# A second standing place for gathered cache values in the MLP, two value products per interruption, and the sampled tokens' norm kept in SBUF

## The chip, the cores and the metric

The kernel runs on one core of a Trainium2 chip. TensorE (called PE in the profile) multiplies; its weight loads are listed apart as PEld. VectorE is DVE, ScalarE is ACT, GpSimd is POOL, and SyncE (SP) issues most transfers. Each engine has its own queue of instructions and works it off in order; engines wait for each other through semaphores. The metric is the device time of one execution in microseconds; less is better.

## The reference

One step of a one-layer decoder on 2048 new prompt tokens and on 64 sampled tokens (8 sequences of 8), all in float32:

```python
z = jnp.einsum('bsd,dc->bsc', x, w_in)              # 1024 -> all projections
fox_h = _fox_prompt(fq, fk, fv, flogf)              # causal attention, 8 heads of 64
(C_p, n_p, m_p), m_h = _mlstm_prompt(mq, mk, mv, ig, lf)
...
k_past = cache_k[l][page_table].reshape(DB, past, FOX_HEADS, FOX_HEAD_DIM)
v_past = cache_v[l][page_table].reshape(DB, past, FOX_HEADS, FOX_HEAD_DIM)
...
s_past = jnp.einsum('bqhd,bkhd->bhqk', q, k_past) * scale + Ln + R
p = jax.nn.softmax(jnp.concatenate([s_past, s_new], axis=-1), axis=-1)
o = jnp.einsum('bhqk,bkhd->bqhd', p[..., :P], v_past) + ...   # sampled attention, 8192 past tokens
...
mix = jnp.concatenate([fox_h, mn], axis=-1) @ w_o
x1 = _layer_norm(DN_ALPHA * x + mix, ln1_g, ln1_b)
hid = jnp.square(jax.nn.relu(x1 @ w1))              # 1024 -> 4096
return _layer_norm(DN_ALPHA * x1 + hid @ w2, ln2_g, ln2_b)
```

The sampled attention reads 8 sequences x 64 pages x 128 tokens of keys and as many of values from a paged cache through a page table: 128 MB each.

## The kernel before, in words

The program has these stages, one after the other: A (input projections), B (prompt attention), O (output projection and first norm, `phase_o`), and C (the MLP and second norm, `phase_c`). The large products are written as three float32r matmuls of 512 columns (`mm3`, L162 to L164): an operand is split into a high and a low part, the high parts made by ACT (`split_hi`, L153) and the low ones by DVE or POOL (`split_lo`, L156).

The sampled attention is a generator, `sample_attention`, that is advanced beside all other work. Its 294 steps (`step(n)`) run in stage A up to step 78 and go on from there in O and C. `tick(us)` is called after each piece of the main work with the TensorE time that the piece is worth; when 4.93 us have come together in O and C, one step is emitted. What a step does is fixed by its number n:

- every fourth step (n % 4 == 2): `qk_step`, the scores of four gathered pieces of keys (tile `sQ`, L1826, 16 matmuls of 32 output rows and 256 columns; the trace has two records for each of them, since they are in float32);
- every second step from 38 on: `pv_step`, the value product of one pair of gathered pieces of values, called a pair below (tile `sO`, L1938, 8 matmuls for each half of the pair in the trace, 16 in all);
- at two steps out of eight: `weights`, which turns four blocks of the softmax's result (tile `sT`, L1895) into `PTs`, the stationary operand of the next four pairs;
- gathers: `k_gather` (L1803) fetches one piece of 128 rows x 4 KB by an indirect DMA on POOL's queue, into a ring of six; `v_gather` (L1914) fetches the two pieces of a pair, 1 MB.

`two_sides`, `mm3` and the narrow matmuls share TensorE's queue, so each step that multiplies interrupts the wide matmuls. The interruptions are called runs here: all that stands on PE between two wide matmuls.

A pair of values needs a place in SBUF. The first place is the two `vt` buffers of the attention's own pool. The second is whatever `vx["more"]()` gives at the time: the tiles `vx` of stage O's pool, and in stage C the two landing buffers `xr`, through which the normed rows x1 also come back from DRAM to be turned (`x1_load`, L1249). Since the landing buffers are needed for that at the end of each of the MLP's four blocks, `vx["more"]` is set to `None` from the seventh of the eight passes of a block to the end of the eighth, and `take_back` emits attention steps until no pair stands in the second place. With no second place, one pair is gathered and consumed at a time.

Stage C works on four blocks of tokens: 512, 512, 512 and 512 + 64 (the sampled tokens, tile 16). For each block `x1_turn` (L1261) puts x1 transposed into `x1h` and `x1l`, `hidden` makes 256 columns of the hidden layer (tile `ph`), and `output` multiplies them with w2 by a seven-product scheme and adds the results to the rows `ys` (tile `y`, L1452). The rows are loaded from DRAM at the start of a block by DMAs on ACT's queue (L1510) and are normed and stored at the start of the next one. They come from a ring of five tiles (`row`), which stage O uses as well.

The sampled tokens' output projection and first norm (`sampled`, `norm_quick`) are done at the end of the third block, after the attention has ended. The normed rows are written to DRAM (L197), loaded again into a landing buffer to be turned, and loaded a third time as the row tile of the fourth block.

The order of instructions on an engine is set by a scheduler that simulates a timeline; `issue_after` holds an instruction behind another.

## Time and profile before

| | |
|---|---|
| median of 3 runs | 3186.63 us (3184.83 to 3199.43) |
| profiled execution, its time | 3196.47 us |
| its span, first to last instruction | 3194.7 us |
| mean granted TensorE clock | 0.99 |
| PE busy | 3107.4 us, 97% of the span |
| DVE / ACT / POOL busy | 65% / 45% / 28% |
| bytes moved by DMA | 732.58 MB, mean 229 GB/s |
| stage O, from the first wide matmul | about 1300 to 1526 us |
| stage C, blocks 1 to 3, with the attention | about 1526 to 2735 us |
| sampled tokens' projection, norm and turn | about 2735 to 2790 us |
| stage C, block 4 | to the end |

Lines of a timeline read: start, duration, engine, line, operation, tiles (out<-in), shape, count, and in brackets the engine's idle time before and what ended it. Lines of a table of waits read: waiting engine, tile and line, what it waited for, microseconds in total, times, the longest.

### The profile page before, as it was taken

The page shows a single profiled execution, that of the slowest core. Times are in us where ns is not written, and L with a number is a line of the kernel's source. Part 1 is how long each engine was busy: PE and PEld are TensorE (multiplying, and loading weights), DVE is VectorE, ACT ScalarE, POOL GpSimd, SP SyncE. Part 2 cuts the span into 40 slices and gives each one's busy share as a digit, 9 for nine tenths or more (in the row PEclk, how much of TensorE's full clock was granted, in tenths as well). Part 3 has the DMA queues.
Part 4 walks back from the last instruction along what each step waited for, and adds up shares of the span by engine and source line. Part 5 has one row for each costly group of instructions (what it writes and reads, how often), then busy time and mean ns, then how long its engine had stood idle before and what let it go on. Part 6 is the DMA issues. An engine that isn't in the chain of part 4 may idle for free. (4 is left out here: it accounts for less than half of the span.)

```text
span 3194.7 us, 53743 instructions
## 1 busy us (share of the span) xinstructions
PE 3107.4 (97%) x19869; PEld 2442.5 (76%) x19869; DVE 2084.9 (65%) x5025; ACT 1438.9 (45%) x2629; POOL 907.6 (28%) x976
## 2 busy tenths in 40 slices
PE   8999999999999999999999999999999999899998
PEld 8997787787766667777677777777767777698886
DVE  6857467465488787534656568565676665766667
ACT  3343244343387777412444455343444444344442
POOL 0121132423443333476333324333333111000000
PEclk9999999999999999999999999999999999999999
DMA  5565665877787765687877879878779766643231
GB/s 191 153 212 183 236 227 201 285 258 241 239 272 176 196 172 133 228 300 250 318 277 284 303 243 341 302 263 315 294 259 342 277 213 208 209 155 133 100 124 63
DMA packets 323614, 732.58 MB, mean 229 GB/s; under 512 B 63096, under 2 KB 153720, under 8 KB 322456
## 3 DMA queue, kind: packets, MB, share of 16 engines
q1 hardware_dynamic: 235928, 413.36, 39.1%
q0 software_dynamic: 83808, 304.91, 27.4%
q10 hardware_dynamic: 3616, 10.88, 0.9%
q8 instruction: 157, 2.57, 0.3%
q14 instruction: 105, 0.86, 0.1%
HBM read 676.20 MB, written 86.38 MB: 239 GB/s over the span
## 5 line engine op out<-in xcount | busy, mean ns | idle before, releaser
L156 DVE TENSOR_TENSOR wl<-wr,wh 128x1024 fp32r<-128x1024 f32 x300 | 366.0, 1222 | 241.4 <-ACT wh L153 235.4
L153 ACT ACTIVATE wh<-wr 128x1024 fp32r<-128x1024 f32 x300 | 315.8, 1055 | 338.8 <-PE py L164 166.0
L162 PE MATMUL ph<-x1h,wh 128*128 128x512 f32 (+1 forms) x1280 | 455.4, 356 | 0.0
L163 PE MATMUL ph<-x1l,wh 128*128 128x512 f32 (+1 forms) x1280 | 453.7, 355 | 0.2 <-DVE x1l L156 0.2
L164 PE MATMUL ph<-x1h,wl 128*128 128x512 f32 (+1 forms) x1280 | 451.8, 355 | 1.0 <-DVE wl L156 0.8
L1803 POOL DMA_INDIRECT kT<-cache_k,idxK x256 | 276.4, 1080 | 556.5 <-PE sQ L1826 491.5
L162 PE MATMUL py<-wh,hh 128*128 128x512 f32 x900 | 357.9, 402 | 5.6 <-DVE y L1452 3.0
L163 PE MATMUL py<-wl,hh 128*128 128x512 f32 x900 | 354.3, 395 | 0.0
L164 PE MATMUL py<-wh,hl 128*128 128x512 f32 x900 | 351.3, 394 | 0.4 <-DVE hl L156 0.4
L1452 DVE TENSOR_TENSOR y<-y,py 128x512 f32<-128x512 f32 x410 | 277.3, 682 | 101.2 <-PE py L164 97.0
L1914 POOL DMA_INDIRECT vt<-cache_v,idxV x164 | 179.0, 1091 | 399.5 <-PE sO L1938 337.6
L162 PEld LDWEIGHTS ph<-x1h,wh 128*128 128x128 f32 x1280 | 241.6, 189 | 40.4 <-issue 7.4
L164 PEld LDWEIGHTS ph<-x1h,wl 128*128 128x128 f32 x1280 | 240.8, 189 | 37.4 <-issue 3.7
L163 PEld LDWEIGHTS ph<-x1l,wh 128*128 128x128 f32 x1280 | 241.6, 189 | 35.2 <-issue 3.7
L162 PE MATMUL pm<-xh,whi 128*128 128x512 f32 (+2 forms) x640 | 230.9, 361 | 0.0
L164 PE MATMUL pm<-xh,wlo 128*128 128x512 f32 (+2 forms) x640 | 228.5, 357 | 0.0
L163 PE MATMUL pm<-xl,whi 128*128 128x512 f32 (+2 forms) x640 | 227.6, 356 | 0.0
L162 PEld LDWEIGHTS py<-wh,hh 128*128 128x128 f32 x900 | 169.2, 189 | 59.3 <-issue 21.2
L162 PE MATMUL pm<-whi,xh 128*128 128x256 f32 (+4 forms) x624 | 202.2, 325 | 8.9 <-ACT whi L153 8.9
L156 DVE TENSOR_TENSOR wlo<-wra,whi 128x1024 fp32r<-128x1024 f32 (+1 forms) x112 | 139.9, 1251 | 100.7 <-ACT whi L153 100.2
L164 PEld LDWEIGHTS py<-wh,hl 128*128 128x128 f32 x900 | 170.5, 189 | 40.0 <-issue 2.1
L163 PE MATMUL pm<-wlo,xh 128*128 128x256 f32 (+4 forms) x624 | 200.1, 321 | 0.6 <-DVE wlo L156 0.6
(378 smaller groups left out, 6495.7 us busy)
## 6 DMA issues: line engine op xcount, KB each, us to landing
wr<-w SPq DMA_DIRECT2D x200, 512.0 KB
wra<-w_in SPq DMA_DIRECT2D x104, 512.0 KB
wr<-dw SPq DMA_DIRECT2D x96, 512.0 KB
dw<-w POOLq DMA_DIRECT2D x48, 512.0 KB, 7.2
Rb<-dR SPq DMA_DIRECT2D x128, 128.0 KB
kT<-dw SPq DMA_DIRECT2D x28, 512.0 KB
kT<-w SPq DMA_DIRECT2D x25, 512.0 KB
xn<-xp_t SPq DMA_DIRECT2D x16, 512.0 KB
```

What stands on the lines that cost most here:

```text
L153: last["ACT"] = A.activation(dst, src, AF.Copy, scale=scale)
L156: r = (eng or V).tensor_tensor(dst, src, hi.bitcast(F32), op=OP.subtract)
L162: T.matmul(ps, wh, xh, start=first, stop=False, skip_group_check=shared)
L163: T.matmul(ps, wh, xl, start=False, stop=False, skip_group_check=shared)
L164: last["PE"] = T.matmul(ps, wl, xh, start=False, stop=stop, skip_group_check=shared)
L1452: V.tensor_tensor(y, y, ps, op=op)
L1803: G.indirect_dma_start(out=piece(n), out_offset=None, in_=ck, in_offset=IO(ap=idxK[:, b, j // 2, j % 2:j % 2 + 1], axis=0))
L1914: vx["last"] = G.indirect_dma_start(out=vt.rearrange("p f c -> p (f c)"), out_offset=None, in_=cv, in_offset=IO(ap=idxV[:, b, (kt % 4) * 4 ...
```

## The change

The change touches stages O and C only; stages A and B issue the same instructions in the same order.

- The ring of output rows has four tiles and a fifth one, `y5`, of its own. Stage O uses `y5` for every fifth row tile. In stage C the blocks use the four of the ring; `y5` is a half of the second place for gathered values and, after the attention's end, the row tile of the sampled tokens.
- `x1h` and `x1l` are 512 columns wide for the first three blocks and 576 for the fourth, for which their pool is closed and opened again. The 4 KB per partition that this leaves hold `vt2`, the other half of the second place.
- In stage C `vx["more"]` is `second`, which hands out `y5` and `vt2` in turn, and is not withdrawn. `take_back` at the blocks' ends is gone (the one at the end of stage O stays).
- At a step with n % 4 == 2 the pair p and, if its gather was emitted at an earlier step, the pair p + 1 are both multiplied, right behind the step's `qk_step`; the step after next then has no pair left to do. `v_gather` is called at most once per step, at each step that has room, instead of as often as there is room at every second step. `weights` may come one step earlier when the previous four pairs are done.
- The sampled tokens' normed rows stay in `y5`: they are turned from there and are block 4's row tile. The write to DRAM and both loads are gone.

```diff
@@ norm_quick
-            e.dma_start(out[:, h[i]], x[:, h[i]])
+            if out is not None:
+                e.dma_start(out[:, h[i]], x[:, h[i]])
@@ phase C
     def row():
-        return C["py"].tile([128, D], F32, name="y", bufs=5)
+        return C["py"].tile([128, D], F32, name="y", bufs=4)
+
+    def fifth():
+        return C["py"].tile([128, D], F32, name="y5", bufs=1)
+
+    def second():
+
+        C["second"] = not C.get("second")
+        return fifth() if C["second"] else C["px"].tile([128, D], F32, name="vt2", bufs=1)
+
+    def x1_pool():
+
+        es_x1.close()
+        C["px"] = es_x1.enter_context(tc.tile_pool(name="px", bufs=1, side="right", reuse_waits="tile"))
...
         if i == 0 and 0 in halves:
-            C["x"] = (C["px"].tile([128, 8, 576], F32R, name="x1h", bufs=1), C["px"].tile([128, 8, 576], F32R, name="x1l", bufs=1))
+            if t == 12:
+                x1_pool()
+            C["x"] = [C["px"].tile([128, 8, 576 if t == 12 else 512], F32R, name=m, bufs=1) for m in ("x1h", "x1l")]
...
-            xs[t] = row()
+            xs[t] = fifth() if t % 5 == 3 else row()
...
+        x1_pool()
+        vx["more"] = second
...
-            y = row()
+            y = C["y16"] = fifth()
...
-            C["normed"] = norm_quick(y[:64], 64, st, *gb, pc, dx1[S:], SY)
+            C["normed"] = norm_quick(y[:64], 64, st, *gb, pc, None)
...
-                    begun.append(x1_load(CB[ci][i + 2]))
+                    t = CB[ci][i + 2]
+                    begun.append(C["y16"] if t == 16 else x1_load(t))
...
-        vx["more"] = landing
...
                     for t in blk:
+                        if t == 16:
+                            ys[t] = C["y16"]
+                            continue
                         ys[t] = row()
...
-                if p == 6:
-                    vx["more"] = None
...
-                    vx["more"] = landing
...
                 if p == 6 and ci < 3:
-                    take_back()
                     begun = [x1_load(t) for t in CB[ci + 1][:2]]
@@ step
         if p is not None and p < 128:
-            pv_step(p // 16, p % 16, after)
+            due = [p] if p >= vx["done"] else []
+            if n % 4 == 2 and vx["at"].get(p + 1, n) + 1 < n:
+                due.append(p + 1)
+            for p in due:
+                after = pv_step(p // 16, p % 16, after)
+                vx["done"] = p + 1
...
-        for hg in range(2):
-            u = at(n, 36 + hg, 8)
-            if u is not None and u < 32:
-                weights(u // 4, u % 4, hg)
+        u, hg = divmod(vx["turned"], 2)
+        if u < 32 and n >= 36 + hg + 8 * u - (1 if u % 4 and vx["done"] >= 4 * u else 0):
+            weights(u // 4, u % 4, hg)
+            vx["turned"] += 1
...
-        if n >= 35 and (n % 2 == (0 if sole else 1) or not vx["live"]):
-            while v_room():
-                v_gather()
+        if n >= 35:
+            if sole:
+                if n % 2 == 0 or not vx["live"]:
+                    while v_room():
+                        v_gather(n)
+            elif v_room():
+                v_gather(n)
```

How the order moves is shown at three places. The first is TensorE's queue in the middle of the MLP's first block, around two of the attention's steps. Before (rows of L162 to L164 are wide matmuls):

```order
L163 MATMUL ph<-x1l,wh 128x512
L164 MATMUL ph<-x1h,wl 128x512
L1826 MATMUL sQ<-kT,qb 32x256 x16
L1938 MATMUL sO<-vt,PTs 32x256 x8
L162 MATMUL ph<-x1h,wh 128x512
L163 MATMUL ph<-x1l,wh 128x512
```

and 46 rows further on

```order
L163 MATMUL ph<-x1l,wh 128x512
L164 MATMUL ph<-x1h,wl 128x512
L1938 MATMUL sO<-xr,PTs 32x256 x8
L1895 MATMUL sT<-ident,S 128x128 x4
L162 MATMUL py<-wh,hh 128x512
L163 MATMUL py<-wl,hh 128x512
```

The first pair stands in the run of the scores, the second in a run of its own with four transposes.

The same scores and pairs in the changed kernel, whose lines from 197 on have moved (L1845 is the scores' line, L1958 the pairs'; `vt_19301` and `y_19299` are `vt2` and `y5`):

```order
L163 MATMUL ph<-x1l,wh 128x512
L164 MATMUL ph<-x1h,wl 128x512
L1845 MATMUL sQ<-kT,qb 32x256 x16
L1958 MATMUL sO<-vt,PTs 32x256 x8
L1958 MATMUL sO<-vt_19301,PTs 32x256 x4
L1958 MATMUL sO<-y_19299,PTs 32x256 x4
L162 MATMUL ph<-x1h,wh 128x512
L163 MATMUL ph<-x1l,wh 128x512
```

The second pair, which had a run of its own together with four transposes, now follows the first in the scores' run. Over stages O and C the order has 118 runs with narrow matmuls before and 80 now; 60 of the 118 hold one pair and no scores, 11 of the 80 do.

The second place is POOL's queue at the end of the MLP's first block, where the second place was withdrawn before (L179 is a step of the rows' norm). Before:

```order
L1803 DMA kT<-cache_k,idxK 128x1024 x4
L1914 DMA vt<-cache_v,idxV 128x1024 x2
L1914 DMA xr<-cache_v,idxV 128x1024
L179 TENSOR_TENSOR ln_rs<-ln_rs,nhalf 128x1 x2
L1914 DMA vt<-cache_v,idxV 128x1024 x2
L179 TENSOR_TENSOR ln_rs<-ln_rs,nhalf 128x1 x2
L1914 DMA vt<-cache_v,idxV 128x1024 x2
L1803 DMA kT<-cache_k,idxK 128x1024 x4
L1914 DMA vt<-cache_v,idxV 128x1024 x2
L1803 DMA kT<-cache_k,idxK 128x1024 x4
L1914 DMA vt<-cache_v,idxV 128x1024 x2
```

And with the change (L1822 gathers keys, L1934 values):

```order
L1822 DMA kT<-cache_k,idxK 128x1024 x4
L1934 DMA vt<-cache_v,idxV 128x1024 x2
L1934 DMA vt_20721<-cache_v,idxV 128x1024
L1934 DMA y_20719<-cache_v,idxV 128x1024
L1822 DMA kT<-cache_k,idxK 128x1024 x4
L1934 DMA vt<-cache_v,idxV 128x1024 x2
L1934 DMA vt_21001<-cache_v,idxV 128x1024
L1934 DMA y_20999<-cache_v,idxV 128x1024
L179 TENSOR_TENSOR ln_rs<-ln_rs,nhalf 128x1 x3
L1822 DMA kT<-cache_k,idxK 128x1024 x4
L1934 DMA vt<-cache_v,idxV 128x1024 x2
L1934 DMA vt_21260<-cache_v,idxV 128x1024
```

Pairs that were gathered one at a time into `vt` alone are gathered two at a time, and the four gathers of keys stand between two pairs and the next two, here as in the rest of stage C.

The third place is ACT's queue at the start of the MLP's second block, where the block's four rows are loaded. Before:

```order
L1510 DMA y<-dx_71 128x1024
L1434 ACTIVATE hq<-ph 128x512
L1510 DMA y<-dx_71 128x1024 x2
L1435 ACTIVATE hq<-hq 128x512
L1510 DMA y<-dx_71 128x1024
L1897 COPY PTs<-sT 128x4x4x8
L153 ACTIVATE hh<-s 128x512
```

With the change:

```order
L1532 DMA y<-dx_71 128x1024
L1453 ACTIVATE hq<-ph 128x512
L1532 DMA y<-dx_71 128x1024
L1454 ACTIVATE hq<-hq 128x512
L153 ACTIVATE hh<-s 128x512
L153 ACTIVATE hh<-hq 128x512
L1453 ACTIVATE hq<-ph 128x512
L153 ACTIVATE hh<-s 128x512
L1532 DMA y<-dx_71 128x1024
```

The third load stands behind five pieces of ACT's other work, and the fourth, six rows further on, behind more, since with a ring of four each of them waits for the store of the row that the tile held.

More of the change, by code (lines that the diff above doesn't have):

```diff
@@ L107, in body @@
     last = {}
-    vx = dict(more=None, live=[], next=0, of={})
+    vx = dict(more=None, live=[], next=0, of={}, at={}, done=0, turned=0)
     kx = dict(ring=None, new=False, free=False)
@@ L1240, in row @@
     def row():
-        return C["py"].tile([128, D], F32, name="y", bufs=5)
+        return C["py"].tile([128, D], F32, name="y", bufs=4)
[4 more added lines that the diff above has]
+        return fifth() if C["second"] else C["px"].tile([128, D], F32, name="vt2", bufs=1)
+    es_x1 = ExitStack()
+    def x1_pool():
+        es_x1.close()
+        C["px"] = es_x1.enter_context(tc.tile_pool(name="px", bufs=1, side="right", reuse_waits="tile"))
     def w1_pieces(fc):
@@ L1348, in phase_o @@
         es_b.close()
-        C["px"] = es_c.enter_context(tc.tile_pool(name="px", bufs=1, side="right", reuse_waits="tile"))
+        x1_pool()
+        vx["more"] = second
         ppx = es_x.enter_context(tc.tile_pool(name="ppx", bufs=1, space=PSUM, side="right", reuse_waits="tile"))
@@ L1659, in body @@
         phase_c()
+        es_x1.close()
         es_c.close()
@@ L1902, in v_new, with v_gather @@
         SY.dma_start(vn, O["v_sample"][0, b].rearrange("t h d -> t (h d)"))
-    def v_gather():
+    def v_gather(n):
         p = vx["next"]
+        vx["at"][p] = n
         b, kt = divmod(p, 16)
@@ L1947, in pv_step @@
             V.tensor_scalar(z["os"], po, z["rl"], None, op0=OP.mult)
+        return after
     def pv_end(b):
```

2 lines of the change are left out of this document (1 added, 1 removed).

## The prediction

> **What bounds the kernel now.** I read the page first: its busy times, and the share of the span.
>
> ```profile
> span 3194.7 us, 53743 instructions
> PE 3107.4 (97%) x19869; PEld 2442.5 (76%) x19869; DVE 2084.9 (65%) x5025; ACT 1438.9 (45%) x2629; POOL 907.6 (28%) x976
> ```
>
> PE is the bound, and no other engine comes near it. What a change in stages O and C can give is therefore of two kinds: PE time that the narrow work costs beyond its own matmuls, and idle time of PE. The order differs only from stage O on and is the same again for the last block of the MLP, so I asked for PE's waits from 1300 to 2740 us, where the attention runs beside O and C.
>
> ```profile
> PE sO L1938 <- DMA vt<-cache_v,idxV: 13.1, 6, 5.6
> ...
> PE sO L1938 <- DMA xr<-cache_v,idxV: 3.5, 3, 2.1
> PE sQ L1826 <- DMA kT<-cache_k,idxK: 3.3, 4, 1.2
> PE sO L1938 <- DMA vx<-cache_v,idxV: 1.2, 1, 1.2
> ...
> PE py L162 <- ACT hh L153: 0.8, 1, 0.8
> ```
>
> The four rows with a cache's name add up to 21.1 us: PE stood still for gathered values (17.8) and keys (3.3). Asked again for 2330 to 2375, the end of the MLP's second block, where the second place is withdrawn and pairs go one by one, the same view has the longest of them:
>
> ```profile
> PE sO L1938 <- DMA vt<-cache_v,idxV: 5.6, 1, 5.6
> ```
>
> The splits of operands by ACT, the last row above, held PE for 0.8 us. So the change can win at most these 21.1 us as idle time, and the rest must come from fewer runs.
>
> The timeline of PE shows what a run costs. A pair alone, scores with one pair, scores with two pairs:
>
> ```profile
> 2018.38 0.39 PE L164 MATMUL ph<-x1h,wl 128*128 128x512 f32 x1
> 2018.70 1.07 PE L1938 MATMUL sO<-vt,PTs 128*32 128x256 f32 x16
> 2019.70 0.50 PE L162 MATMUL ph<-x1h,wh 128*128 128x512 f32 x1
> 2020.05 0.40 PE L163 MATMUL ph<-x1l,wh 128*128 128x512 f32 x1
> ```
> ```profile
> 1812.35 0.39 PE L163 MATMUL ph<-x1l,wh 128*128 128x512 f32 x1
> 1812.57 0.39 PE L164 MATMUL ph<-x1h,wl 128*128 128x512 f32 x1
> 1812.89 1.93 PE L1826 MATMUL sQ<-kT,qb 128*32 128x256 f32 x32
> 1814.64 1.05 PE L1938 MATMUL sO<-vt,PTs 128*32 128x256 f32 x16
> 1815.62 0.50 PE L162 MATMUL ph<-x1h,wh 128*128 128x512 f32 x1
> 1815.96 0.40 PE L163 MATMUL ph<-x1l,wh 128*128 128x512 f32 x1
> ```
> ```profile
> 1479.25 0.39 PE L163 MATMUL pw<-wl,mh 128*128 128x512 f32 x1
> 1479.56 1.93 PE L1826 MATMUL sQ<-kT,qb 128*32 128x256 f32 x32
> 1481.32 1.05 PE L1938 MATMUL sO<-vx,PTs 128*32 128x256 f32 x16
> 1482.18 1.05 PE L1938 MATMUL sO<-vt,PTs 128*32 128x256 f32 x16
> 1483.15 0.50 PE L164 MATMUL pw<-wh,ml 128*128 128x512 f32 x1
> 1483.49 0.40 PE L162 MATMUL pw<-wh,mh 128*128 128x512 f32 x1
> ```
>
> Wide matmuls overlap, so I count from start to start. In an undisturbed stream they start 0.225 us apart (1812.35 to 1812.57, and the same over longer stretches: 0.227). From the last wide matmul before a run to the second one behind it, less two such steps, the run of one pair costs 2020.05 - 2018.38 - 0.45 = 1.22 us, scores with one pair 1815.96 - 1812.57 - 0.45 = 2.94, and scores with two pairs 1483.49 - 1479.25 - 0.45 = 3.79. Scores with one pair and another pair by itself are 4.16, in one run 3.79: **a run saved is worth 0.37 us**, the price of leaving the wide stream and coming back to it. The pair's own matmuls cost the same in either place.
>
> **Part by part. Runs.** Counted through the order of stages O and C, runs with narrow matmuls go from 118 to 80: 38 x 0.37 = 14.1 us less. The 80 include what goes against the change: some 15 pieces of a pair that stand alone, because the scheduler's timeline has its second half arrive late. Transposes that stood in a pair's run stand alone more often, 46 runs of them instead of 31. What such a run costs to enter lies between nothing and the 0.37 of a narrow one; since transposes are 128 wide like the main stream, I take 0.1, 1.5 us in all. Net of both: **-12.6 us**, and between -8.5 (0.37 for each) and -14.
>
> **Waits for values.** Of the 21.1 us, what is left? Both pairs of a run are released together now, and POOL's queue gathers four pieces of keys, then four of values, in every period. How long that takes is seen where the old kernel did nearly the same, at the end of the second block:
>
> ```profile
> 2345.07 2.72 POOL L1803 DMA_INDIRECT kT<-cache_k,idxK  x1 [25.74 <-PE sQ L1826]
> 2353.71 0.94 POOL L1914 DMA_INDIRECT vt<-cache_v,idxV  x1 [0.30 <-issue]
> 2365.60 1.93 PE L1938 MATMUL sO<-vt,PTs 128*32 128x256 f32 x16 [5.62 <-DMA vt<-cache_v,idxV]
> ```
>
> The sixth gather is issued 8.6 us after the first, and its data are there when PE goes on, 11.9 us later. The DMA view from 1300 to 2740 gives the median from issue to landing:
>
> ```profile
> vt<-cache_v,idxV POOLq DMA_INDIRECT x120, 9.9
> xr<-cache_v,idxV POOLq DMA_INDIRECT x78, 10.4
> ```
>
> With eight gathers at 1.24 us each (0.94 and 0.30 of the second row), the last is issued 8.7 us after the first and lands some 10 to 12 us later. The first is issued 1.4 us after the run's first matmul:
>
> ```profile
> 1742.14 1.93 PE L1826 MATMUL sQ<-kT,qb 128*32 128x256 f32 x32
> 1743.52 0.94 POOL L1803 DMA_INDIRECT kT<-cache_k,idxK  x1 [13.24 <-PE sQ L1826]
> 1762.72 1.93 PE L1826 MATMUL sQ<-kT,qb 128*32 128x256 f32 x32
> 1792.31 1.93 PE L1826 MATMUL sQ<-kT,qb 128*32 128x256 f32 x32
> ```
>
> so the second pair is complete 20 to 22 us after its predecessor's run began. It is needed when the next run has done scores (1.76) and the first pair (0.86), 2.6 us after that run's start (the rows from 1479.56 to 1482.18). A wait arises where two runs start less than 17.5 to 19.5 us apart. In the old trace two neighbours start 20.6 and 29.6 us apart, as the last rows show; in the new order, at 0.227 us a wide matmul and the run prices above, most neighbours lie 22 to 30 us apart, five at 18 to 20, and six, where a new sequence begins, at 11 to 15; at those the order lets most pairs follow the scores at some distance. I expect 1 us at each of the five and a third of one at each of the six, 7 us in all, so this term is **-14 us**. Its bounds are -21 (nothing is late) and -5 (1.5 us are lost at each of the eleven).
>
> The Trainium skill, in "DMA: Bandwidth & Descriptors", section "Anatomy of one DMA — SWDGE (gpsimd) path", puts a gather's time at 2.0 us plus its bytes over 436 GB/s. By that page an estimate for eight pieces of 512 KB in a row is 11.6 us from first issue to last landing, and no pair would be late; the sixth took 20.5 us here, so the page's figure does not hold in this company of weight loads, and the sum goes by the rows.
>
> **Rows in a ring of four.** At the start of a block the last row's load, on ACT's queue, now waits for a store that is issued when the block's last norm is done, and ACT's work behind it waits too. At the second block the timeline has SP's store of the last row and ACT's last load (before the change) beside each other:
>
> ```profile
> 1966.26 0.34 SPq L1609 DMA_DIRECT2D y_prompt<-y  x1
> 1967.14 0.65 ACTq L1510 DMA_DIRECT2D y<-dx  x1
> ```
>
> With a few microseconds for the store, that load would come 2 to 3 us later. The new order has put it behind nine pieces of ACT's work there. Two products of `output` are made ahead, so a short hold of ACT need not reach PE; without that cover it would be three starts of blocks at 2 us. I take **+1 us**, between 0 and +6.
>
> **The sampled tokens.** The write and the two loads go. While they ran, PE waited for DVE, not for the row's DMA (waits over the whole span, then DVE's timeline):
>
> ```profile
> PE py L162 <- DVE y L1452: 3.0, 1, 3.0
> 2758.78 1.40 DVE L194 SCALAR_TENSOR_TENSOR y<-y,ln_m,g 64x512 f32<-64x512 f32 x2
> 2760.09 1.40 DVE L196 SCALAR_TENSOR_TENSOR y<-y,ln_r,b 64x512 f32<-64x512 f32 x2
> ```
>
> The norm's four instructions hold DVE for 2.6 us and they stay, at the same place of its queue. I take 0 for this part; the removed transfers, 256 KB each, could give 1 us at most. Stage O's use of the fifth tile keeps the ring's period of five: 0.
>
> Sum: -12.6 - 14 + 1 = -25.6 us. The profiled execution would go from 3196.47 to 3170.9; it lies 9.8 us above the median of the runs, 3186.63, which would go to **3161 us**.
>
> **Rivals.** *The waits stay.* If gathers that are released together come later than I read, the 21 us stay in new places, at the second pair of each run, and only the runs' gain is left: 3186.6 - 12.6 + 1 = 3175 us. For it: eight gathers in a row take 20 to 22 us and periods are hardly longer. Against it: the bytes per period are the same, and the pair that was late at the blocks' ends is no longer alone. *The runs give nothing*, if 0.37 us is an accident of three places: 3186.6 - 14 + 1 = 3174. Against it: each of the three costs is read from matmul starts without a wait. *No pair is late at all*, if rows of eight land faster than the burst of 2345 us did: 3186.6 - 12.6 - 21.1 + 1 = 3154 us. The Trainium skill's page above would have it so. *Slower*: POOL's queue is in order, and the power of each row's norm (L179) now stands behind both pairs' gathers, not one; ACT's scaling of the row (L181) waits for it, and the splits of the operands queue behind that. The waits of the whole span have
>
> ```profile
> ACT y L181 <- DVE ln_rs L180: 69.0, 21, 12.1
> ```
>
> so ACT is held there already, by up to 12 us, of which PE felt 0.8 us at most in the stretch above. The groups of 1300 to 2740 us count the norms that stand beside gathers:
>
> ```profile
> L179 POOL TENSOR_TENSOR ln_rs<-ln_rs,nhalf 128x1 f32<-128x1 f32 x24 | 18.4, 766 | 30.1 <-DVE ln_rs L178 21.6 <-DMA vt<-cache_v,idxV 4.6 <-ACT hq L1434 3.6
> ```
>
> If each of the 24 cost PE more than 1.07 us, the gain of 25.6 would be gone; at 2 us it is 3186.6 - 25.6 + 48 = 3209 us. Against it: POOL waits less in the new order, since it no longer holds a gather for a pair that goes alone some 10 us later. *That it does not do what it says*, pairs still going one by one, is excluded by the order but for the 11 lone pairs counted.
>
> **How the numbers follow.** Forecast (3152 to 3170 with its unknown terms) 0.62, waits stay 0.18, runs give nothing 0.06, no pair late 0.08, slower 0.06. About 0.5%, 16 us, is what a measurement of this kernel can tell from no change. Faster than 3170.7 are nearly all of the forecast (0.56) and of "no pair late" (0.08) and a small part of the two cases at 3174 (0.05): 0.69. Slower by as much is the last rival where it is strong: 0.05. The rest, 0.26, is no change. The range from 3150 to 3180 leaves out the slower cases and the tails.
>
> **What would show it.** In the changed profile the waits of PE for `vt`, `vt2` and `y5` from 1300 to 2740 us should add up to 3 to 14 us, the largest at the second pair of a run, and none of 5 us at the blocks' ends; a lone pair should still cost 1.2 us and scores with two pairs 3.8; the stretch from the first `pw` to the last pair should be some 25 us shorter, and the stretch behind it equally long. More than 20 us of such waits, or waits of PE for ACT's `hh` and `wh` beyond 5 us, would make the forecast wrong, the first by the gathers, the second by POOL's queue or the rows' loads.

## The result, and the profile after

The changed kernel took 3173.22 us (median of 8 runs, 3160.63 to 3179.66), the kernel before 3188.11 us beside it (8 runs, 3179.93 to 3199.43). The ratio is 0.9946 with a 95% interval of 0.993 to 0.9962: about 17 us faster, where 25.6 were forecast. The profiled execution took 3172.96 us. Its page begins:

```profile
span 3171.3 us, 53742 instructions
PE 3088.1 (97%) x19869; PEld 2447.1 (77%) x19869; DVE 2077.7 (66%) x5025; ACT 1435.7 (45%) x2629; POOL 901.9 (28%) x976
```

TensorE (PE) has the same 19869 matmul records and is busy 19.3 us less; no other engine is near to being the bound. A run of scores with two pairs, from PE's timeline:

```profile
1825.15 0.39 PE L163 MATMUL py<-wl,hh 128*128 128x512 f32 x1
1825.38 0.39 PE L164 MATMUL py<-wh,hl 128*128 128x512 f32 x1
1825.69 1.93 PE L1845 MATMUL sQ<-kT,qb 128*32 128x256 f32 x32
1827.44 1.48 PE L1958 MATMUL sO<-vt,PTs 128*32 128x256 f32 x24
1828.74 0.61 PE L1958 MATMUL sO<-y,PTs 128*32 128x256 f32 x8
1829.29 0.50 PE L162 MATMUL py<-wh,hh 128*128 128x512 f32 x1
1829.62 0.40 PE L163 MATMUL py<-wl,hh 128*128 128x512 f32 x1
```

By the prediction's way of counting it costs 1829.62 - 1825.38 - 0.45 = 3.79 us, as it did before; it now stands in 26 places instead of 4. PE's waits from 1300 to 2720 us, those with a cache's name:

```profile
PE sO L1958 <- DMA vt<-cache_v,idxV: 15.5, 8, 5.0
...
PE sQ L1845 <- DMA kT<-cache_k,idxK: 1.3, 2, 1.0
...
PE sO L1958 <- DMA y<-cache_v,idxV: 0.4, 2, 0.2
```

They add up to 17.2 us, against 21.1 before. So the waits, which were to give 14 us, gave 3.9.

To compare executions I split the time from the first wide matmul of stage O (`pw`) to PE's last one into three parts: idle time in front of a matmul; runs, which is all from a run's first matmul to the fourth wide one behind it, less idle time and less the ordinary steps of the wide matmuls in it; and the rest, the wide stream. The stream is the same work everywhere and still came out between 1503.8 and 1511.0 us, so a difference of that size in one execution's total says nothing.

| kernel | sum, us | idle | runs (number of all kinds) | wide stream | waits for cache values and keys |
|---|---|---|---|---|---|
| before | 1882.3 | 37.3 | 334.3 (194) | 1510.7 | 21.1 |
| changed | 1861.2 | 33.0 | 318.8 (178) | 1509.4 | 17.2 |
| changed, profiled again | 1861.6 | 32.9 | 320.4 (178) | 1508.3 | 16.1 |
| pairs apart | 1874.6 | 31.4 | 334.0 (193) | 1509.2 | 16.5 |
| place withdrawn | 1881.5 | 48.4 | 325.2 (171) | 1507.9 | 23.5 |
| sampled tokens through DRAM | 1857.4 | 34.9 | 318.7 (178) | 1503.8 | 17.4 |
| values first | 1857.1 | 30.5 | 315.6 (170) | 1511.0 | 13.8 |
| scores earlier | 1853.6 | 30.8 | 314.5 (168) | 1508.3 | 13.5 |
| both | 1844.8 | 27.4 | 311.7 (166) | 1505.7 | 9.9 |
| both, all values | 1840.8 | 23.3 | 309.0 (165) | 1508.5 | 6.0 |

From before to changed: runs -15.5, idle -4.3, stream -1.3, in all -21.1. Two things limit what these parts can say. The profiled execution of the kernel before, 3196.47 us, lies 8 us above its median, so the parts add up to more than the 15 to 17 us between the medians. And the border between runs and stream is drawn by choice: counted from the last wide matmul before a run to the fourth behind it, with 0.227 us taken off for each wide matmul of 512 columns and 0.13 for each of 288, the same two traces give -13.7 for the runs and -3.1 for the stream.

Of the 17.2 us, 11.7 stand in front of the first pair behind a run's scores, 4.2 in front of the second, and 1.3 are for keys. The longest wait is at the end of the MLP's first block, where a new sequence begins. The rows are of PE and POOL, in order of time:

```profile
1900.81 1.94 PE L1845 MATMUL sQ<-kT,qb 128*32 128x256 f32 x32
1902.18 1.00 POOL L1822 DMA_INDIRECT kT<-cache_k,idxK  x1 [22.92 <-PE sQ L1845]
1909.09 0.94 POOL L1934 DMA_INDIRECT vt<-cache_v,idxV  x1 [0.30 <-issue]
1912.58 0.93 POOL L1934 DMA_INDIRECT y<-cache_v,idxV  x1 [0.30 <-issue]
1914.65 1.93 PE L1845 MATMUL sQ<-kT,qb 128*32 128x256 f32 x32
1921.55 1.93 PE L1958 MATMUL sO<-vt,PTs 128*32 128x256 f32 x16 [4.96 <-DMA vt<-cache_v,idxV]
1928.08 0.64 PE L1958 MATMUL sO<-vt,PTs 128*32 128x256 f32 x8
```

Two runs follow each other after 13.8 us. The sixth of the eight gathers between them is issued at 1909.09 and is there at 1921.55, 12.5 us later and 19.4 us after the first was issued. The run before these two lies 45.5 us back: the first scores of a sequence come late, and the next run keeps its time. The five neighbours of this kind (10.9 to 14.0 us apart) hold 12.6 us of the 17.2.

They do not share it evenly, and the closest two have the least of it. One of these, 10.9 us apart, reads on PE:

```profile
1693.09 1.93 PE L1845 MATMUL sQ<-kT,qb 128*32 128x256 f32 x32
1703.97 1.07 PE L1845 MATMUL sQ<-kT,qb 128*32 128x256 f32 x16
1712.67 1.50 PE L1958 MATMUL sO<-vt,PTs 128*32 128x256 f32 x24
```

Here the order has put the first pair 8.7 us behind the start of the run, 19.6 us behind the start of the run before, and it waits for nothing. At 1914.65 it stands right behind the scores, 15.8 us behind the start of the run before (1921.55 less the wait of 4.96). So the distance that counts is not that from run to run, but that from the start of one run to the place of the next run's first pair.

### The profile page after: what moved, and what is told of

Same layout as the page of the kernel before. It is cut to its first block, busy times and chain, and to the rows that moved or that the text cites. A ratio compares the mean times of both kernels' runs of the same rounds, so it can differ in the third digit from the quotient of the medians.

```text
span 3171.3 us, 53742 instructions
## 1 busy us (share of the span) xinstructions
PE 3088.1 (97%) x19869; PEld 2447.1 (77%) x19869; DVE 2077.7 (66%) x5025; ACT 1435.7 (45%) x2629; POOL 901.9 (28%) x976
## 4 chain that ended last, share of the span: by engine, by line
PE 82%; DMA 8%; DVE 4%; issue 3%; POOL 1%; ACT 1%; SPq 0%; DVEq 0%; POOLq 0%; ACTq 0%
PE ph L164 7%; PE ph L162 7%; PE ph L163 7%; PE py L162 6%; PE py L164 6%; PE py L163 6%; PE pm L162 5%; PE pm L164 5%; PE pm L163 5%; PE po L1087 4%; PE sO L1958 3%; PE pt L1077 3%; PE sQ L1845 3%; DMA vt<-cache_v,idxV 3%; PE pS L1032 2%
## 5 line engine op out<-in xcount | busy, mean ns | idle before, releaser
L153 ACT ACTIVATE wh<-wr 128x1024 fp32r<-128x1024 f32 x300 | 315.6, 1055 | 324.9 <-PE ph L163 148.3
L162 PE MATMUL ph<-x1h,wh 128*128 128x512 f32 (+1 forms) x1280 | 454.3, 355 | 0.2 <-ACT x1h L153 0.2
L164 PE MATMUL ph<-x1h,wl 128*128 128x512 f32 (+1 forms) x1280 | 449.8, 355 | 0.4 <-DVE wl L156 0.2
L1822 POOL DMA_INDIRECT kT<-cache_k,idxK x256 | 272.3, 1064 | 619.0 <-PE sQ L1845 554.5
L162 PE MATMUL py<-wh,hh 128*128 128x512 f32 x900 | 356.3, 401 | 5.5 <-DVE y L1471 3.7
L164 PE MATMUL py<-wh,hl 128*128 128x512 f32 x900 | 351.4, 394 | 1.2 <-DVE hl L156 1.2
L1934 POOL DMA_INDIRECT vt<-cache_v,idxV x197 | 209.5, 1063 | 399.0 <-PE sO L1958 324.5
L164 PEld LDWEIGHTS ph<-x1h,wl 128*128 128x128 f32 x1280 | 240.7, 189 | 37.9 <-issue 4.9
L162 PEld LDWEIGHTS ph<-x1h,wh 128*128 128x128 f32 x1280 | 241.5, 189 | 36.5 <-issue 4.5
L162 PE MATMUL pm<-xh,whi 128*128 128x512 f32 (+2 forms) x640 | 231.2, 361 | 0.0
L164 PE MATMUL pm<-xh,wlo 128*128 128x512 f32 (+2 forms) x640 | 228.6, 357 | 0.0
L162 PEld LDWEIGHTS py<-wh,hh 128*128 128x128 f32 x900 | 169.0, 189 | 54.2 <-issue 15.9
L162 PE MATMUL pm<-whi,xh 128*128 128x256 f32 (+4 forms) x624 | 201.9, 324 | 8.9 <-ACT whi L153 8.9
L164 PEld LDWEIGHTS py<-wh,hl 128*128 128x128 f32 x900 | 170.1, 189 | 40.3 <-issue 2.5
```

Source lines behind the costliest of these rows:

```text
L153: last["ACT"] = A.activation(dst, src, AF.Copy, scale=scale)
L162: T.matmul(ps, wh, xh, start=first, stop=False, skip_group_check=shared)
L164: last["PE"] = T.matmul(ps, wl, xh, start=False, stop=stop, skip_group_check=shared)
L1822: G.indirect_dma_start(out=piece(n), out_offset=None, in_=ck, in_offset=IO(ap=idxK[:, b, j // 2, j % 2:j % 2 + 1], axis=0))
L1934: vx["last"] = G.indirect_dma_start(out=vt.rearrange("p f c -> p (f c)"), out_offset=None, in_=cv, in_offset=IO(ap=idxV[:, b, (kt % 4) * 4 ...
```

## The experiments

Theory A: the gain is the runs, and the waits that stay come from bursts of eight gathers between runs that stand close together. The main rival, B: the gain is the second place that is never withdrawn, and the runs give nothing. The numbers of narrow runs in the expectations are of the whole order and include the scores of new keys and one run at the end of stage B, so they read 124 and 87 where the prediction has 118 and 80.

**Pairs apart.** One part of the change undone:

```diff
-            if n % 4 == 2 and vx["at"].get(p + 1, n) + 1 < n:
-                due.append(p + 1)
```

> The change as it stands, but a pair is never taken two to a run: each even pair stands alone again, as in the kernel before. The second place (fifth output row and the room beside turned x) and the sampled tokens' new way are kept. Narrow runs in the instruction order: 124 as in the kernel before, against 87 in the changed kernel. Theory A (the gain of the change is the runs, 0.37 us each): about 37 x 0.37 = 13.7 us come back in the runs; because only six gathers then stand behind one run instead of eight, waits for gathered keys and values are 5 to 15 us instead of 17.2; sum +3 to +12 over the changed kernel, a ratio of 0.996 to 0.999 to the kernel before. Theory B (the gain is that the second place is never withdrawn, and the runs give nothing): the same ratio as the changed kernel or less, 0.991 to 0.995, with waits of 10 us or less.

Measured: 3181.69 us, ratio 0.9996 to the kernel before (0.9983 to 1.001). The gain is gone. The table says by what: the runs are back at 334.0, 15.2 us over the changed kernel for 37 narrow runs, 0.41 us each, and the waits are hardly other than the changed kernel's. Theory A's waits of 5 to 15 us were set a little too low, and so was its ratio of 0.996 to 0.999; theory B, which expected the changed kernel's ratio, is out:

```profile
PE sO L1958 <- DMA vt<-cache_v,idxV: 8.7, 4, 3.8
PE sO L1958 <- DMA y<-cache_v,idxV: 3.8, 2, 1.9
...
PE sQ L1845 <- DMA kT<-cache_k,idxK: 3.1, 3, 1.8
...
PE sO L1958 <- DMA vx<-cache_v,idxV: 0.9, 1, 0.9
```

**Place withdrawn.** Two pairs per run, but the second place is what it was:

```diff
-        vx["more"] = second
+        vx["more"] = landing
...
+                if p == 6:
+                    vx["more"] = None
...
+                    vx["more"] = landing
...
+                    take_back()
```

> The change as it stands, but the second place is again the two landing buffers of the tokens' rows, which is withdrawn at the end of each block and drained, as in the kernel before. Two pairs per run are kept, as are the sampled tokens' new way. Narrow runs in the instruction order: 86, against 87 in the changed kernel and 124 in the kernel before. Theory A (the gain is the runs): nearly all of the gain stays, ratio 0.994 to 0.998 to the kernel before; the difference to the changed kernel is that of the waits for gathered values alone, which at the ends of blocks return (5 us each at most three times, 17 to 30 us in all against 17.2). Theory B (the gain is the place): ratio 0.999 to 1.001, that of the kernel before.

Measured: 3184.86 us, ratio 0.9997 (0.9985 to 1.0009). This is theory B's number and not theory A's, but not for theory B's reason: the runs are still 9.1 us cheaper than in the kernel before, and idle time has grown by 11.1 us, which eats it. The waits from 1300 to 2720 us:

```profile
PE sO L1962 <- DMA vt<-cache_v,idxV: 14.9, 5, 7.4
PE px L1279 <- DMA xr<-dx: 7.7, 1, 7.7
PE sO L1962 <- DMA xr<-cache_v,idxV: 6.6, 4, 2.5
PE sQ L1849 <- DMA kT<-cache_k,idxK: 1.7, 2, 1.2
```

The second row is a row that is to be turned. The two landing buffers held a pair until 1902.9 us; the first two rows were loaded then, and this one at 1923.3, when the buffer had been turned once. The 7.4 of the first row stand at the start of the second block, in a run that follows another after 15.2 us. So I had undersized what the place does: with either half of the change alone the time is that of the kernel before. Without the second pair in a run the runs cost what they did, and without the lasting place what the runs save is paid back in waits.

**Sampled tokens through DRAM.** Only the sampled tokens' way is undone:

```diff
-            C["normed"] = norm_quick(y[:64], 64, st, *gb, pc, None)
+            C["normed"] = norm_quick(y[:64], 64, st, *gb, pc, dx1[S:], SY)
...
-                    begun.append(C["y16"] if t == 16 else x1_load(t))
+                    begun.append(x1_load(t))
...
-                        if t == 16:
-                            ys[t] = C["y16"]
-                            continue
-                        ys[t] = row()
+                        ys[t] = fifth() if t == 16 else row()
```

> The change as it stands, but the sampled tokens' normed rows go through DRAM again (stored, loaded to be turned, loaded once more as residual). Theory A (this part was hidden work): the ratio to the kernel before is that of the changed kernel, 0.993 to 0.996, and the profiled stretch from the first of the sampled tokens' products to the end is within 2 us of the changed kernel's. Rival C (the part of the change that shows is this one): +5 us or more over the changed kernel, ratio 0.996 or more, with TensorE waiting for a turned x or a loaded row around the sampled tokens.

Measured: 3167.18 us, ratio 0.9944 (0.9922 to 0.9966), the changed kernel's. PE's wait for the norm (`PE py <- DVE y`) is 4.9 us in all against 3.7, the waits for gathers are the same, and the stretch from the sampled tokens' first product to the end is 450.7 us against 451.6. The three transfers were hidden work. The profile's sum is 3.8 us lower, but that is in the wide stream.

**Values first.** POOL's order within a run is changed:

```diff
-            k_gather(n)
+            with ExitStack() as es:
+                if n % 4 < 2:
+                    es.enter_context(tc.issue_after(vx["last"].ins))
+                k_gather(n)
```

> The change as it stands, but GpSimd issues the last two key gathers of a run behind the run's four value gathers: two keys, four values, two keys instead of four keys, four values. By the order of instructions 79 narrow runs against 87. Theory A1 (waits are set by how long all eight gathers of a run take together, about 20 us, where runs follow each other closer than that): the waits move from values to keys and their sum stays at 14 to 20 us (17.2 in the changed kernel); the time changes only by the runs, 8 x 0.37 = 3 us less. Theory A2 (the values wait because they stand last in a queue, and keys land with time to spare): waits for values fall to 8 us or less, those for keys stay under 4 us, and the time falls by 8 to 12 us, a ratio of 0.991 to 0.992 to the kernel before.

Measured: 3172.1 us, ratio 0.9958 (0.9945 to 0.9971). Neither form was right. The waits did not move to the keys, which wait for nothing now, and did not fall to 8 us either:

```profile
PE sO L1958 <- DMA vt<-cache_v,idxV: 8.6, 7, 2.5
PE sO L1958 <- DMA y<-cache_v,idxV: 5.2, 2, 3.6
```

13.8 us in all, 3.4 less than in the changed kernel, and runs 3.2 us cheaper. The ratio does not tell it from the changed kernel. The edit moved more than POOL's queue: the scheduler also put the first pairs of the five close neighbours 12.8 to 15.7 us behind the start of the run before, where the changed kernel has them at 15.8 to 19.6, so what the order on POOL saves was in part given away again.

**Scores earlier.** If distance is the cause, two close neighbours that are drawn apart should stop waiting. The score buffer in PSUM is one; before a new sequence's first scores it serves four others, in the order of the program. Two of these are moved behind:

```diff
-        b = at(n, 69, 32)
+        b = at(n, 71, 32) if n < 293 else 7
         if b is not None:
             pv_end(b)
-        b = at(n, 37, 32)
+        b = at(n, 39, 32)
         if b is not None and b < 8:
             softmax_new(b)
             v_new(b)
```

The changed kernel was timed again in the same session, as a base for this and the next ones:

> The changed kernel itself, timed once more beside the next ones so that they can be set against it: a ratio of 0.994 to 0.996 to the kernel before, 17 to 18 us of waits for gathered values and keys in the attention stretch.

Measured: 3170.03 us, ratio 0.9938 (0.9921 to 0.9955), 16.1 us of waits.

> The change as it stands, with one more: of the four users of the one score buffer in PSUM that stand ahead of a new sequence's first scores, two (the turning of the last sequence's sums, and of its probabilities for the new tokens) are put two steps later, behind these scores. In the changed kernel the instruction order has 158 to 208 matmuls of the block before those scores and 29 to 38 behind them, so that the next run follows 11 to 14 us later; with this edit it is 128 to 161 before and 38 to 75 behind, and 73 narrow runs against 87. Theory D (the waits that are left are those of runs that follow each other closer than their eight gathers take, and they come so close because the first scores of a sequence are late): waits for values and keys fall from 17.2 to 4 to 9 us, with 14 x 0.37 = 5 us for the runs the time falls by 13 to 18 us against the changed kernel, a ratio of 0.989 to 0.991 to the kernel before. Rival E (the waits belong to the shared DMA rings in the block's stream and come whatever the distance): 15 us or more of waits stay, and the time falls by the 5 us of the runs at most, a ratio of 0.993 to 0.995.

Measured: 3163.86 us, ratio 0.9921 (0.9907 to 0.9934): 6 us less than the changed kernel beside it, between what theory D and rival E said. Runs are 4.3 us cheaper than in the first profile of the changed kernel, and 13.5 us of waits are left. Neighbour by neighbour the trace is clearer than the sum. Four of the five pairs of neighbours at the starts of sequences moved from 10.9, 10.9, 11.6 and 14.0 us to 21.4, 21.9, 21.6 and 23.8 us, and none of them waits. The fifth is still 16.7 us apart and waits 5.2 us; a new close pair came up:

```profile
1734.70 1.93 PE L1845 MATMUL sQ<-kT,qb 128*32 128x256 f32 x32
...
1747.12 2.12 PE L1845 MATMUL sQ<-kT,qb 128*32 128x256 f32 x32
1755.35 1.93 PE L1958 MATMUL sO<-vt,PTs 128*32 128x256 f32 x16 [6.11 <-DMA vt<-cache_v,idxV]
```

It is 12.4 us apart and waits 6.1 us. These two hold 11.3 of the 13.5. Besides, PE waits 3.4 us for a row to be turned (`px <- xr`), which it did not in the changed kernel.

Two other neighbours, 15.6 and 15.8 us apart, wait 0.5 us or less, so the distance of runs is not all. The place of the first pair sorts them. Behind the start of the run before, it stands at 25.0 and 21.3 us in these two, and at 14.5 and 18.6 us in the two that wait. In the changed kernel it stands at 15.8, 18.4 and 19.1 us where the first pair waits at a close neighbour, and at 19.0 and 19.6 where it does not. Of the first pairs that stand further off, 21.0 us and more, two wait there: one at 21.6 us, for 0.8, and one at 26.1 us, for 2.9. At that last one two of the values' gathers took 19 and 20 us from issue to landing; why was not tried.

**Half of the keys' bytes, two ways.** What makes a burst of eight take 20 us? First, half of the tokens of each key gather, then half of each row:

```diff
+        w = 128 if n < NA + 6 else 64
+        G.indirect_dma_start(out=piece(n)[:w], ..., in_offset=IO(ap=idxK[:w, ...], axis=0))
```

> The change as it stands, but every key gather beyond the first 82 fetches the rows of 64 tokens instead of 128: the other half of those keys is left out, so the output is not the reference's. Orders and distances are unchanged, eight gathers a run move 3 MB instead of 4. Theory D (a run waits because its eight gathers together take about 20 us): the last value lands about 5 us sooner after the first issue, and the waits for values fall from 15.9 us to 6 or less. Rival F (values are late because they are issued late, when the pairs before have left their places, and each then takes its 10 us whatever stands before it): the waits stay at 12 us or more.

```diff
+            G.indirect_dma_start(out=piece(n)[:, 0:512], out_offset=None, in_=ck.rearrange("r (h c) -> (r h) c", h=2), ...)
```

> The change as it stands, but every key gather beyond the first 82 fetches 2 KB for each of its 128 rows instead of 4 KB (of other rows; half of each key tile keeps what it held), so the output is not the reference's. The order of instructions and the distances between runs are those of the kernel with half the tokens of the key gathers, which also moved half the bytes, on 64 partitions, and had 31.9 us of waits. Theory D (the burst's bytes set the wait, and 64 partitions did not shorten it since those rows went through half of the rings): waits for values fall to 8 us or less, a value lands 9 to 10 us after its issue also in the close neighbours. Rival F (each value takes what it takes from its own issue, whatever the keys ahead of it weigh): waits of 12 us or more, values 12 to 17 us after their issue in the close neighbours.

Measured: 3198.71 us with half of the tokens, 3165.16 us with half of the rows, one run each. Contrary to the first expectation the order did not stay as it was: the scheduler reckons with shorter gathers, makes 72 narrow runs, the same in both, and puts pairs nearer to the scores: at the close neighbour that was shown at 1703.97 us the first pair stood 8.7 us behind the run's start and stands 1.9 to 2.0 us behind it now. So the two can be compared with each other, but with the changed kernel only by single gathers. The transfers from 1300 to 2720 us, first with half of the tokens, then with half of the rows:

```profile
q0 software_dynamic: 44544, 157.05, 36.7%
```
```profile
q0 software_dynamic: 44448, 156.79, 31.2%
```

The columns are packets, MB and share of 16 engines' time: nearly the same packets and bytes take less time when they go to all 128 partitions, in rows of 2 KB, than to 64 in rows of 4 KB. Which of the two differences does it was not tried. The waits are 31.9 us with 64 partitions and 19.5 us with half rows, in both cases rival F's number (12 or more) and not theory D's; but the pairs stand nearer to the scores, so these sums do not decide. With half rows the same neighbours at the end of the first block, 13.9 us apart, read:

```profile
1898.26 1.05 POOL L1825 DMA_INDIRECT kT<-cache_k,idxK  x1 [25.51 <-PE sQ L1849]
1905.22 0.95 POOL L1938 DMA_INDIRECT vt<-cache_v,idxV  x1 [0.30 <-issue]
1914.39 1.07 PE L1962 MATMUL sO<-vt,PTs 128*32 128x256 f32 x16 [1.69 <-DMA vt<-cache_v,idxV]
```

The sixth gather is there 9.2 us after its issue instead of 12.5, and 16.1 us after the first issue instead of 19.4. Over the whole stretch a gather into `vt` landed 7.4 us after its issue at the median, against 10.7 in the changed kernel. So rival F, by which a value's 12 us do not depend on the keys ahead of it, is out, and theory D's landing time came (9 to 10 us), though not its waits. Of the 3 MB up to the sixth gather 1 MB was left out, and 3.3 of 19.4 us went with it. If the other bytes weigh as much, all 3 MB are worth some 10 us, about half of the burst; that is an estimate. The rest would be the issues on POOL, 6.96 us to the sixth, and what a gather takes whatever its size. Theory D's reason for the run with 64 partitions, that those rows went through half of the rings, no run here shows.

**Both edits.** Scores earlier and values first together, then with the last two key gathers behind all four values:

> The scores of a new sequence taken earlier, and the last two key gathers of a run issued behind its four value gathers, together; 72 narrow runs. If distance is what counts (theory D), the order of issue adds nothing: within 3 us of the kernel with the earlier scores alone, a ratio of 0.988 to 0.991 to the kernel before. If the order of issue counts as well, 4 us or more less than that one, and no wait for values over 1.5 us left.

```diff
+            vx["both"] = vx.get("both", [])[-1:]
...
+            vx["both"].append(vx["last"])
...
-                    es.enter_context(tc.issue_after(vx["last"].ins))
+                    for i in vx["both"]:
+                        es.enter_context(tc.issue_after(i.ins))
```

> The scores of a new sequence taken earlier, and the last two key gathers of a run issued behind all four of its value gathers; in the kernel with both edits before, the fourth value gather (into the fifth output row) still stood behind them, and its pair is the one that waited (8.6 of 9.9 us). If the place in the queue is what is left, that wait falls to 4 us or less and keys wait for 2 us at most: 3 to 6 us less than that kernel, a ratio of 0.987 to 0.989 to the kernel before. If distance alone is left, the waits move to the keys and the ratio stays at 0.989 to 0.990.

Measured: 3154.02 us, ratio 0.9894 (0.9879 to 0.9909), for both; 3152.68 us, ratio 0.9887 (0.9869 to 0.9904), with all values ahead. The first is 16 us faster than the changed kernel timed beside it, 10 us more than the earlier scores alone, and each of its four executions is faster than all six of those: the place in the queue counts as well as the distance. Of the 8.8 us between the two traces, idle time is 3.4, runs are 2.8 and the stream 2.6. The expectation that no wait over 1.5 us would be left did not hold: the waits of the fourth value are 8.6 us in all, the longest 4.7. The second version takes most of that away, but its time cannot be told from the first's. Its page and its waits for the cache:

```profile
span 3151.1 us, 53760 instructions
PE 3079.9 (98%) x19869; PEld 2447.5 (78%) x19869; DVE 2074.5 (66%) x5025; ACT 1436.8 (46%) x2629; POOL 908.7 (29%) x976
...
PE sO L1960 <- DMA vt<-cache_v,idxV: 3.2, 3, 1.4
PE sO L1960 <- DMA y<-cache_v,idxV: 2.8, 1, 2.8
```

6.0 us of waits and 309.0 us of runs: this version beats both kernels, by 1.1% the one before and by 0.5 to 0.6% the changed one. The latter is a quotient of ratios from different sessions (0.9887 / 0.9938 and 0.9887 / 0.9946), since the two were not timed side by side.

## Why the prediction was right, and where it was wrong

The direction and the range held; the predicted time was 12 us too low, and 3173 us is nearer to the rival *the waits stay* (3175 us, a chance of 0.18) than to the forecast. The range, 3150 to 3180 us, takes in that rival too, so that it held says nothing about the waits; the runs were right in mechanism and size, while of the waits it had the cause, bursts between close runs, and not the size. By its steps:

- *Runs, -12.6 us, between -8.5 and -14.* Right. The profiles have -15.5 and, with the second profile of the changed kernel, -13.9. Taking the second pair out of the run again brought 15.2 us back. The price of 0.37 us for a run, read from three places, was a good measure: 0.41 over 37 runs (0.35 if the border of a run is drawn the other way that was given above).
- *Waits for values, -14 us, between -21 and -5.* This is the step that failed, and it failed in its size: -3.9, outside the bounds. The six close neighbours and the five at 18 to 20 us were counted rightly. Two things were not. First, the working follows the second pair, which is complete "20 to 22 us after its predecessor's run began" and needed 2.6 us behind the next run's start. But the first pair is needed 1.76 us behind it already, and its gathers were later than the same working would have them: with the first gather issued 1.4 us after the predecessor's start, the sixth 6.2 us after the first, and 10 to 12 us more to land, the first pair would have been there 17.6 to 19.6 us after the predecessor's start, and where it waited in the five it was there after 19.5 to 21.0. So the largest waits stand at the first pair and not, as the signs had it, at the second. Second, the price of the six neighbours at 11 to 15 us, "a third of one each". The five of them at starts of sequences cost 0.1, 1.0, 5.0, 3.3 and 3.2 us, 2.5 on average. That the order "lets most pairs follow the scores at some distance" was true, by 5.1 to 8.7 us at four of the five, but it is enough only where the sum of both distances reaches some 19 to 20 us. At 1914.65 it had put off the second pair alone (to 1928.08), while the first stood right behind the scores and waited 5.0 us. The sixth neighbour, 15.1 us apart, waited for nothing, and those at 18 to 20 us, priced at 1 us each, cost 2.9 at one of 18.3 us and 0.9 or less at the others. The 17.2 us lie between the 3 to 14 that the signs named and the 20 that would have made the forecast wrong.
- *Rows in a ring of four, +1 us.* About 0: from 1300 to 2720 us the 0.8 us for ACT's `hh` are gone from PE's list of waits, and 0.8 us for DVE's `hl` stand in it instead.
- *Sampled tokens, 0.* Right, by the experiment that undid it.
- *None of 5 us at the blocks' ends.* Wrong: the longest wait, 4.96 us, stands at the end of the first block. It is not the wait of before (one place for pairs); it comes with the late first scores of a sequence. With these taken earlier the runs there are 16.7 us apart and still wait 5.2 us, so at this place itself the cause is not shown by removing it, as it is at the four others.
- *The stretch to the last pair 25 us shorter, the one behind it equally long.* It is 31.0 us shorter (1398.7 against 1429.7) and the one behind 9.8 us longer (462.9 against 453.1): the attention ends earlier in the program, with 2400 wide matmuls still to come instead of 2354. The two must be taken together, -21.2.
- *Slower, by the norms behind the gathers.* ACT's wait for the norm (`y <- ln_rs`) went from 69.0 to 71.3 us, and PE did not feel it. *No pair is late* fell: the seventh gather of a burst landed 19.2 us after the first one's issue at the median in the changed kernel (33 bursts; the eighth has no landing in its trace), the eighth 21.6 us in the kernel before (10 bursts). The Trainium skill's figure in "DMA: Bandwidth & Descriptors", section "Anatomy of one DMA — SWDGE (gpsimd) path", from which 11.6 us had been estimated, does not hold here.

Not foreseen at all was that the two halves of the change need each other, which the two experiments that undo one of them show: 0.9996 and 0.9997.

## What to carry to other kernels

Interruptions of a stream can be priced from a few places of the timeline and counted through the order; that product held to 3 us. Waits for bursts of transfers must be priced at the closest neighbours, one by one, and not by the mean distance, and there from the issue of the burst to the place in the order of the first instruction that needs it. One instruction that comes late makes the next run close; evening out those few places, with the values ahead of the keys that are needed later, gave as much again as the whole change. When two edits share a buffer, undo each alone before saying which of them gives the gain.

## What the runs showed that was not expected

A long wait costs more than its idle time. Busy times around the wait of 4.96 us in the changed kernel, by stretches (the third number from the end is the granted clock of TensorE):

```profile
1912.00:1915.00 3.00, 3.00 (x20) 2.14 (x22) 3.00 (x6) 1.62 (x3) 1.21 (x2) 1.00 1.01 353
1915.00:1921.50 6.50, 1.59 (x32) 0.68 (x24) 5.03 (x15) 0.82 (x1) 4.56 (x4) 0.80 1.03 411
1921.50:1925.00 3.50, 3.45 (x22) 2.08 (x23) 0.00 (x0) 0.43 (x1) 2.14 (x3) 0.50 1.03 421
1925.00:1930.00 5.00, 5.00 (x30) 3.20 (x33) 2.67 (x4) 1.57 (x3) 1.04 (x2) 0.92 1.03 420
```

Behind the wait the clock was 0.50 for some 4 us: the pair of 1921.55 took 1.93 us where 1.05 is usual, and wide matmuls behind it started 0.43 us apart instead of 0.23, until about 1925.6. That is about 4.1 x (1 - 0.23 / 0.43) = 1.9 us on top of 5.0, and it stands in no column of waits. After most waits of 1.6 to 2.9 us in this profile the next matmuls kept their usual length, but not after two that stood close together: behind 1.86 us (until 2347.31) and 1.37 us (until 2349.74) the clock was 0.50 again, from 2349.8 to 2354 and beyond. Added up from 1312 to 2715 us, the clock stood at 0.50 for 17.1 us in the kernel before and for 17.1 in the changed one, so it has no part in the gain; with the place withdrawn it was 30.7 us, with both edits 6.8. The Trainium skill, "TensorE: Matmul & The Clock Gate", section "Part 1: The HAM clock gate (the "warmup" mystery)", says that the clock halves after an idle window of about 3.4 us; the trace agrees, with 4.96 us of idle and 0.50 behind it. The two waits that stood close together reach 3.23 us only in sum, with 1.1 us of matmuls between them.

A gather of half the rows onto 64 partitions was not as cheap as one of half rows onto 128: at nearly the same packets and bytes the gathers' queue took 36.7% of the DMA engines' time against 31.2%. How the sixteen engines shared this work no run here shows, since the profile has their mean alone.
